# Retention's output product as block pairs of seven products, with the gates ahead of it and weight sums made partly by DMA

## The chip, the cores and the metric

One Trainium2 chip; the kernel runs on one of its cores. The metric is the device time of one execution in microseconds, the median of several runs. TensorE multiplies, VectorE and ScalarE do the elementwise work, SyncE (SP) starts nearly all the DMAs, and GpSimd (POOL) starts some in the changed kernel.

## The reference

Two layers on 512 tokens of width 1024, all float32. Cut to what matters here:

```python
h = rmsnorm(x, g_mix)
z = h @ w_in                      # attention q,k,v | retention q,k,v,g | gate_a | gate_b
ya = sliding_window_sink_attention(aq, ak, av, sinks) @ w_a
r = chunkwise_retention(rq, rk, rv)                       # 4 heads of 256 columns
r = r * lax.rsqrt(jnp.mean(r * r, axis=-1, keepdims=True) + EPS)
r = r.reshape(B, S, RET_V) * jax.nn.silu(rg)              # 512 x 1024
yb = r @ w_b                                              # 1024 x 1024
mixed = jax.nn.sigmoid(ga) * ya + jax.nn.sigmoid(gb) * yb
x = x + mixed @ w_out
h2 = rmsnorm(x, g_mlp)
x = x + jnp.square(jax.nn.relu(h2 @ w_up)) @ w_down       # 4096 hidden columns
```

After the second layer a last rmsnorm follows.

## The kernel before

Activations lie transposed: 8 tiles of 128 features by 512 tokens. For accuracy every float32 operand is split into a high and a low part (`split`: ScalarE copies the source into the high part, VectorE subtracts it for the low part, the "remainder"), and `products` makes of each product three matmuls: high by high, high by low and low by high (lines 280, 281 and 282). Weights come in units of 128 x 1024 elements (512 KB). `unit_order` writes their order out by hand. `unit` hands out the next one and sees to it that the next two are split (`split_until`), which in turn sees to loads further ahead (`load_until`). Loads go into three `raw` tiles, splits into three pairs of `hi` and `lo` tiles, so a load waits on SP's queue until the tile's last reader is done. The order of the instructions on each engine's queue is settled by a scheduler when the kernel is built; each queue then runs in order.

Three shapes of loop use the units. `group` fills four banks of PSUM at once, with the eight input tiles k as its outer loop; `chunk` makes one output tile of 512 tokens from one unit (24 matmuls of 512 columns); `two_chunks` makes two from two units. There are five banks for products.

`pair` makes two output tiles of `w_up` (256 output features by 512 tokens) by a 2 x 2 block scheme with seven products of blocks instead of eight: the blocks are 512 input features by 256 tokens, each product is 4 x 3 matmuls of 256 columns, and three banks a, e and b gather them. Its inputs are blocks of x and four sums of blocks of x (`sum_input`: four additions or subtractions on VectorE, then a split, for each half of the features), its weights are seven blocks, of which some are sums. `load_part` loads the two units of a pair and `add_part` forms the sums with four additions on VectorE of 512 columns each, in `raw` and in large temporary tiles (`big`). A pair comes as four parts for `unit`: three full ones and a half.

The order within a layer, from the retention on: the last values of the retention; `w_in` chunks for the retention's gate (`put_rg`) and for the first four gates `gb` (`gate`), with the retention's second half of the heads woven in between (`advance`, `drain`); a `group` of `w_b`; four more gate chunks; four chunks of `w_b`. `put_mixed` multiplies the result by the gate, adds the attention's share (kept in x's place) and splits the sum into slots `ms`. Then x is loaded back by DMA, from the input or from a copy in DRAM (`spill`), and a group and four chunks of `w_out` add to it. `put_x` also scales and splits each tile of x for the MLP (`scaled_input`, into `xh` and `xl`, with which all products of `w_in` and `w_up` work) and adds up its squares. The MLP begins with a `group` of `w_up`, with `sum_input` and the norm's statistics in its hooks, then two pairs; then 24 turns of a `two_chunks` of `w_down` and a pair in the two layers together; at the end comes a group and chunks of `w_down`.

Of the kernel before, what the change touches and what calls it, by code (L numbers as in the profile page):

```python
# [48 lines left out]
DELAY = 2  # L49


def unit_order():

    order = [("w_in", i) for i in range(4 + 2 + 8 + 2 + 4 + 2)]
    order += [("w_in", i) for i in range(22, 26)]
    order += [("w_a", i) for i in range(4)]
    order += [("w_in", i) for i in range(26, 42)]
    order += [("w_b", i) for i in range(4)]
    order += [("w_in", i) for i in range(42, 46)]
    order += [("w_b", i) for i in range(4, 8)]  # L60
    order += [("w_out", i) for i in range(8)]
    for what, q, i in mlp_sequence():
        if what == "first":
            order += [("w_up", u) for u in range(4)]
        elif what == "pair":
            order += [("pair", 8 * q + 2 * i, part) for part in range(4)]
# [48 lines left out]
def decoder(ctx, tc, xT, x_first, w_in, w_a, w_b, w_out, w_up, w_down, tables, decay, band, out):  # L115
# [17 lines left out]
    def big(name, dtype=F32):  # L133
        return tmp.tile([P, 2, T], dtype, tag="big", name=name, bufs=6)
# [27 lines left out]
    def raw_tile():  # L162
        return wpool.tile([P, UNIT], F32, tag="raw", name="raw")
# [28 lines left out]
    def load_part(i):  # L192
        layer, _, j, part = order[i]
        if part == 0:
            raws[i] = raw_tile()
            nc.sync.dma_start(raws[i][:, LEFT], w_up[layer, j][:, LEFT])
            raws[i + 3] = raw_tile()
            nc.sync.dma_start(raws[i + 3], w_up[layer, j + 1])
        elif part == 1:
            raws[i] = big("raw2").rearrange("p a t -> p (a t)")  # L200
            nc.sync.dma_start(raws[i][:, RIGHT], w_up[layer, j][:, RIGHT])

    def add_part(i):
        part = order[i][3]
        if part == 0:
            w2 = raws[i + 3]
            nc.vector.tensor_tensor(raws[i][:, RIGHT], w2[:, RIGHT], w2[:, LEFT], ALU.add)
        elif part == 1:
            w1 = raws[i - 1]
            nc.vector.tensor_tensor(raws[i][:, LEFT], w1[:, RIGHT], w1[:, LEFT], ALU.subtract)  # L210
        elif part == 2:
            raws[i] = big("raw3").rearrange("p a t -> p (a t)")
            w1, w2, z2 = raws[i - 2], raws[i + 1], raws[i - 1]
            nc.vector.tensor_tensor(raws[i][:, LEFT], w1[:, LEFT], w2[:, RIGHT], ALU.subtract)
            nc.vector.tensor_tensor(raws[i][:, RIGHT], z2[:, RIGHT], z2[:, LEFT], ALU.subtract)

    def split_until(n):
        while state["split"] < min(n, len(order)):
            i = state["split"]
            load_until(i + 3)  # L220
# [10 lines left out]
            for at in (LEFT,) if paired and order[i][3] == 3 else halves(i):  # L231
# [5 lines left out]
            raws.pop(i - 3 if paired else i, None)  # L237
# [76 lines left out]
    def chunk(name, layer, moving, evacuate, rate=1.0):  # L314
# [6 lines left out]
        products(ps, pairs[: n // 2], True, False)  # L321
        advance(rate)
        products(ps, pairs[n // 2 :], False, True)
        evacuate(ps)

    def group(name, layer, moving, evacuates, meanwhile=None):
# [3 lines left out]
        for u in range(4):  # L330
            hi, lo = unit(name, layer)
            for j in range(2):
                k = 2 * u + j
                for c, ps in enumerate(banks):
                    cols = slice(j * T + c * P, j * T + (c + 1) * P)
                    products(ps, [((hi[:, cols], lo[:, cols]), moving[k])], k == 0, k == KD - 1)
# [5 lines left out]
    def two_chunks(name, layer, moving, evacuates):  # L342
# [9 lines left out]
        for ps, evacuate in zip(banks, evacuates):  # L352
            evacuate(ps)

# [125 lines left out]
    def layer_body(layer):  # L480
# [276 lines left out]
        rg, rg_next = {}, {}  # L757

        def put_rg(i):
            def put(ps):  # L760
                if i % 2 == 0:
                    two = big("z")
# [14 lines left out]
        ret = {}  # L777
# [7 lines left out]
        class Head:  # L785
# [53 lines left out]
            def finish(self):  # L839
                h = self.h  # L840
                for e in range(2):
# [5 lines left out]
                    ret[2 * h + e] = (hi, lo)  # L847
# [69 lines left out]
        def gate_tile(c):  # L917
            if c % 2 == 0:
                two = big("gb")
                gates.extend(two[:, j, :] for j in range(2))  # L920

        for c in range(4):
            gate_tile(c)
            chunk("w_in", layer, xs, gate(gates[c]))
        drain()


        ms = {}

        def put_mixed(c):  # L930
            def put(ps):
                m = temp("m")
                nc.vector.tensor_tensor(m, ps, gates[c], ALU.mult)
                nc.vector.tensor_tensor(m, m, mixed[c], ALU.add)
                hi, lo = slots.one(), slots.one()
                split(view(hi), view(lo), m)
                ms[c] = (hi, lo)

            return put

        rT = [tuple(view(s) for s in ret[k]) for k in range(KD)]
        group("w_b", layer, rT, [put_mixed(c) for c in range(4)])
        for c in range(4, KD):
            gate_tile(c)
            chunk("w_in", layer, xs, gate(gates[c]))
        for c in range(4, KD):
            chunk("w_b", layer, rT, put_mixed(c))
        for k in range(KD):
            slots.give(*ret.pop(k))
# [3 lines left out]
        for c in range(KD):  # L953
# [10 lines left out]
        mT = [tuple(view(s) for s in ms[k]) for k in range(KD)]  # L964
# [3 lines left out]
        for k in range(KD):  # L968
            slots.give(*ms.pop(k))
# [5 lines left out]
        H = T // 2  # L975
        sums = [slots.four() for _ in range(4)]
        by_form = [t[0].rearrange("p a (b t) -> p (a b) t", t=H) for t in sums]

        def sum_input(ks):
# [6 lines left out]
            (b11, b12), (b21, b22) = ((t[:, :, :H], t[:, :, H:]) for t in b)  # L986
            f = [big("sums").rearrange("p a (b t) -> p (a b) t", t=H) for _ in range(2)]
            t1, t2, t3, t4 = f[0][:, 0:2, :], f[0][:, 2:4, :], f[1][:, 0:2, :], f[1][:, 2:4, :]
            hi, lo = by_form[ks // 2], by_form[2 + ks // 2]
            nc.vector.tensor_tensor(t1, b12, b11, ALU.subtract)  # L990
            nc.vector.tensor_tensor(t2, b22, t1, ALU.subtract)
            split(hi[:, 0:4, :], lo[:, 0:4, :], f[0])
            nc.vector.tensor_tensor(t3, b22, b12, ALU.subtract)
            nc.vector.tensor_tensor(t4, b21, t2, ALU.subtract)
            split(hi[:, 4:8, :], lo[:, 4:8, :], f[1])

        def form(j):
            return [tuple(by_form[2 * i + k // 2][:, 2 * j + k % 2, :] for i in range(2)) for k in range(4)]

        def block(half, tokens):  # L1000
            at = slice(tokens * H, tokens * H + H)
            return [(xh[:, k, at], xl[:, k, at]) for k in range(4 * half, 4 * half + 4)]
# [20 lines left out]
        def pair(q):  # L1023
            def multiply(ps, weights, left, moving, start=True):
                hi, lo = weights
                cols = [slice((0 if left else 4 * P) + k * P, (0 if left else 4 * P) + (k + 1) * P) for k in range(4)]
                products(ps, [((hi[:, c], lo[:, c]), m) for c, m in zip(cols, moving)], start, True, not start)

            a, e, b = (bank(ps_mm, "mm")[:, :H] for _ in range(3))
            eu, z = temp("eu"), big("z")
            part = unit("pair", layer)
            multiply(a, part, True, block(0, 0))
            nc.scalar.activation(b, a, AF.Copy)  # L1037
            multiply(e, part, False, form(0))
            nc.scalar.activation(eu[:, :H], e, AF.Copy)
            part = unit("pair", layer)  # L1040
            multiply(b, part, True, form(1), False)
            nc.scalar.activation(eu[:, H:], b, AF.Copy)
            multiply(a, part, False, block(1, 0), False)
            nc.vector.scalar_tensor_tensor(z[:, 0, :H], a, 0.0, rms_mlp.value[:, :H], ALU.max, ALU.mult)  # L1044
            part = unit("pair", layer)
            multiply(b, part, True, form(2), False)
            nc.vector.tensor_tensor(z[:, 1, H:], b, eu[:, :H], ALU.add)
            multiply(e, part, False, block(1, 1), False)
            nc.vector.tensor_tensor(z[:, 0, H:], e, eu[:, H:], ALU.add)
            part = unit("pair", layer)  # L1050
            multiply(b, part, True, form(3), False)
            later = rms_mlp.value[:, H:].unsqueeze(1).broadcast_to([P, 2, H])
            nc.vector.scalar_tensor_tensor(z[:, :, H:], z[:, :, H:], 0.0, later, ALU.max, ALU.mult)
            nc.vector.scalar_tensor_tensor(z[:, 1, :H], b, 0.0, rms_mlp.value[:, :H], ALU.max, ALU.mult)
            hi, lo, own = up_home()
            for i in range(2):
# [197 lines left out]
```

## Time and profile before

| | |
|---|---|
| time, median of 3 runs | 1512.68 us (1511.04 to 1513.27) |
| span of the profiled execution | 1511.4 us; the page gives no other time for this execution |
| TensorE busy | 1499.2 us (99%), 8080 matmuls |
| VectorE busy | 1026.7 us (68%) |
| ScalarE busy | 740.1 us (49%) |
| POOL busy | 2.9 us |
| moved by DMA | 155.10 MB, mean 103 GB/s |
| granted clock | 0.998 |

Busy shares are means over the span; what bounds a stage is read from windows, and from the waits in them. [...] In a view of groups a row has the line, the engine, the operation, the tile written and those read, the shape, the count, then busy time and mean duration, and behind the second bar the idle time just before and what ended it. In a view of waits a row has the waiting line, what it waited for, the total, the number and the longest.

### The profile page before, as it was taken

The numbers are of one execution on the slowest core, as the hardware profiler recorded it, in microseconds if no ns is written. First come the engines' busy times: TensorE is split into PE (matmuls) and PEld (weight loads), VectorE is DVE, ScalarE is ACT, GpSimd is POOL, SyncE is SP. The second block draws the span as 40 slices with busy tenths as digits, with TensorE's granted clock in tenths as the row PEclk, the third lists the DMA queues.
The fourth block names the chain that finished last, engine by engine and source line by source line (L and its number), as shares of the span: only waits on it lengthen the run. The fifth ranks groups of instructions, "written<-read, shape, count | busy, mean of one in ns | idle before, by whom it ended". The sixth has DMA issues, their size and how long they took to land.

```text
span 1511.4 us, 20498 instructions
## 1 busy us (share of the span) xinstructions
PE 1499.2 (99%) x8080; PEld 1302.2 (86%) x8080; DVE 1026.7 (68%) x1598; ACT 740.1 (49%) x1163; POOL 2.9 (0%) x13
## 2 busy tenths in 40 slices
PE   9999999999999999999999999999999999999997
PEld 7888888888888999989888888888888999889997
DVE  6877668754787666676678765777449866666664
ACT  6656455632564444444455742555327544444452
POOL 0000000000000000000000000000000000000000
PEclk9999999999999999999999999999999999999999
DMA  6422322233223232233442222222342232232331
GB/s 217 123 97 75 98 79 91 70 125 126 98 78 104 98 112 97 93 104 115 165 131 93 84 84 98 82 79 84 126 125 98 85 104 92 99 111 98 103 108 56
DMA packets 52640, 155.10 MB, mean 103 GB/s; under 512 B 6208, under 2 KB 8384, under 8 KB 52544
## 3 DMA queue, kind: packets, MB, share of 16 engines
q1 hardware_dynamic: 52400, 153.54, 30.6%
q8 instruction: 63, 1.03, 0.3%
q14 instruction: 33, 0.27, 0.1%
q10 hardware_dynamic: 144, 0.26, 0.0%
HBM read 146.96 MB, written 4.19 MB: 100 GB/s over the span
## 4 chain that ended last, share of the span: by engine, by line
PE 98%; ACT 1%; DVE 0%; DMA 0%; issue 0%; DVEq 0%
PE mm L280 29%; PE mm L281 29%; PE mm L282 29%; PE rv L280 2%; PE rv L281 2%; PE rv L282 2%; PE score L651 1%; PE pT L616 1%; PE r L281 1%; PE r L282 1%; PE r L280 1%; PE pv L637 0%; PE pv L636 0%; PE ssq L374 0%; PE ret L281 0%; PE ret L282 0%
## 5 line engine op out<-in xcount | busy, mean ns | idle before, releaser
L235 ACT ACTIVATE hi<-raw 128x1024 fp32r<-128x1024 f32 (+1 forms) x313 | 314.6, 1013 | 517.9 <-PE mm L281 430.6
L236 DVE TENSOR_TENSOR lo<-raw,hi 128x1024 fp32r<-128x1024 f32 (+1 forms) x314 | 362.6, 1164 | 162.0 <-ACT hi L235 161.1
L281 PE MATMUL mm<-r,hi 128*128 128x512 f32 (+1 forms) x1136 | 392.5, 346 | 0.0
L280 PE MATMUL mm<-r,hi 128*128 128x512 f32 (+1 forms) x1136 | 389.5, 346 | 1.0 <-ACT mm L1037 1.0
L282 PE MATMUL mm<-r,lo 128*128 128x512 f32 (+1 forms) x1136 | 388.5, 346 | 0.0
L280 PE MATMUL mm<-xh,hi 128*128 128x512 f32 (+1 forms) x1008 | 358.2, 357 | 0.9 <-ACT xh L290 0.9
L281 PE MATMUL mm<-xl,hi 128*128 128x512 f32 (+1 forms) x1008 | 356.8, 356 | 0.0
L282 PE MATMUL mm<-xh,lo 128*128 128x512 f32 (+1 forms) x1008 | 355.4, 356 | 0.0
L280 PEld LDWEIGHTS mm<-r,hi 128*128 128x128 f32 x1136 | 214.8, 189 | 27.8 <-ACT mm L1037 1.4
L281 PEld LDWEIGHTS mm<-r,hi 128*128 128x128 f32 x1136 | 215.3, 189 | 26.3
L282 PEld LDWEIGHTS mm<-r,lo 128*128 128x128 f32 x1136 | 215.0, 189 | 25.7
L280 PEld LDWEIGHTS mm<-xh,hi 128*128 128x128 f32 x1008 | 191.1, 190 | 27.1 <-ACT xh L290 1.6
L281 PEld LDWEIGHTS mm<-xl,hi 128*128 128x128 f32 x1008 | 191.3, 190 | 25.5
L282 PEld LDWEIGHTS mm<-xh,lo 128*128 128x128 f32 x1008 | 191.0, 190 | 25.5
L1064 DVE TENSOR_TENSOR x<-x,mm 128x512 f32<-128x512 f32 x56 | 37.8, 687 | 34.2 <-PE mm L282 34.2
L282 PE MATMUL rv<-hi,xl 128*128 128x512 f32 x128 | 49.8, 389 | 0.0
L281 PE MATMUL rv<-lo,xh 128*128 128x512 f32 x128 | 49.8, 389 | 0.0
L280 PE MATMUL rv<-hi,xh 128*128 128x512 f32 x128 | 49.4, 391 | 0.0
L281 PE MATMUL mm<-ulo,hi 128*128 128x512 f32 (+1 forms) x128 | 46.3, 363 | 0.0
L280 PE MATMUL mm<-uhi,hi 128*128 128x512 f32 (+1 forms) x128 | 46.2, 362 | 0.0
L282 PE MATMUL mm<-uhi,lo 128*128 128x512 f32 (+1 forms) x128 | 45.7, 365 | 0.0
L1044 DVE SCALAR_TENSOR_TENSOR z<-mm,rstd 128x256 f32<-128x256 f32 x28 | 11.9, 425 | 42.0 <-PE mm L282 42.0
(188 smaller groups left out, 1682.1 us busy)
## 6 DMA issues: line engine op xcount, KB each, us to landing
raw<-w_in_in SPq DMA_DIRECT2D x89, 512.0 KB, 3.3
raw<-w_down_in SPq DMA_DIRECT2D x64, 512.0 KB, 3.3
raw<-w_up_in SPq DMA_DIRECT2D x36, 512.0 KB, 3.3
raw<-w_up_in SPq DMA_DIRECT2D x56, 256.0 KB, 2.7
raw<-w_b_in SPq DMA_DIRECT2D x16, 512.0 KB, 3.2
raw<-w_out_in SPq DMA_DIRECT2D x16, 512.0 KB, 3.5
raw<-w_a_in SPq DMA_DIRECT2D x8, 512.0 KB, 3.3
x<-xT_in SPq DMA_DIRECT2D x15, 256.0 KB, 3.6
```

Source lines behind the costliest of these rows:

```text
L235: nc.scalar.activation(hi[:, at], raw[:, at], AF.Copy)
L236: nc.vector.tensor_tensor(lo[:, at], raw[:, at], f32(hi[:, at]), ALU.subtract)
L280: nc.tensor.matmul(ps, ah, bh, start=start and i == 0, stop=False, **more)
L281: nc.tensor.matmul(ps, ah, bl, start=False, stop=False, **more)
L282: nc.tensor.matmul(ps, al, bh, start=False, stop=stop and i == n - 1, **more)
L616: nc.tensor.transpose(pt[:, i * P : (i + 1) * P], sm[:, at : at + P], ident)
L651: nc.tensor.matmul(ps[:, g * w : (g + 1) * w], q_s[g][:, c, at], part[:, keys], start=i == 0, stop=i == 1)
L1044: nc.vector.scalar_tensor_tensor(z[:, 0, :H], a, 0.0, rms_mlp.value[:, :H], ALU.max, ALU.mult)
L1064: nc.vector.tensor_tensor(x[:, c, :], x[:, c, :], ps, ALU.add)
```

## The change

The product with `w_b` no longer runs as a group and four chunks, but as four pairs of output tiles with the scheme of seven products that the MLP uses; so `pair` is made general, and what is done with its banks is given by a `Sink` (`Up` for the MLP, `Mixed` here). For it the retention's result before its split is kept (`zs`), and `Forms`, made from `sum_input`, forms the four sums of its blocks between the gate chunks. All eight gate chunks come ahead of the pairs. `Mixed` writes the split sum into `xh` and `xl`, which the gates were the last to read; the products of `w_out` read it there, its group with the input tiles in the order in which the pairs make them (`OUT_TILES`). The splits of x for the MLP, which go into the same tiles, can only follow the last chunk of `w_out`, and are made there behind each product (`used`).

The signs in the scheme are turned so that each sum of weight blocks is an addition. Per pair, two of the four are made by VectorE (`add_part`, parts 1 and 2) and two by accumulating DMAs on POOL's queue on top of a plain load (`load_part`, parts 0 and 2). Some blocks are loaded twice for it: 1792 KB for a pair where it was 1024 KB. This holds for the 28 pairs of the MLP and the 8 of `w_b`. There are five `raw` tiles instead of three, loads start four units ahead of a split instead of three, and eight `big` tiles instead of six; the space reserved for POOL's DMA descriptors is 2048 bytes of a partition. The layouts of the weights in DRAM follow.

```diff
+AHEAD = 4
+B_PAIRS = (0, 4, 2, 6)
+OUT_TILES = (0, 1, 4, 5, 2, 3, 6, 7)
...
-    order += [("w_in", i) for i in range(26, 42)]
-    order += [("w_b", i) for i in range(4)]
-    order += [("w_in", i) for i in range(42, 46)]
-    order += [("w_b", i) for i in range(4, 8)]
+    order += [("w_in", i) for i in range(26, 46)]
+    order += [("pair", "w_b", c, part) for c in B_PAIRS for part in range(4)]
...
     def load_part(i):
-        layer, _, j, part = order[i]
+        layer, _, name, j, part = order[i]
+        two = [weights[name][layer, j + a] for a in range(2)]
+        raws[i] = raw = raw_tile()
         if part == 0:
-            raws[i] = raw_tile()
-            nc.sync.dma_start(raws[i][:, LEFT], w_up[layer, j][:, LEFT])
-            raws[i + 3] = raw_tile()
-            nc.sync.dma_start(raws[i + 3], w_up[layer, j + 1])
+            nc.sync.dma_start(raw, two[0])
+            nc.gpsimd.dma_start(raw[:, RIGHT], two[1][:, LEFT], accum_op=ALU.add)
         elif part == 1:
-            raws[i] = big("raw2").rearrange("p a t -> p (a t)")
-            nc.sync.dma_start(raws[i][:, RIGHT], w_up[layer, j][:, RIGHT])
+            nc.sync.dma_start(raw[:, RIGHT], two[1][:, RIGHT])
+        elif part == 2:
+            nc.sync.dma_start(raw[:, LEFT], two[0][:, LEFT])
+            nc.gpsimd.dma_start(raw[:, LEFT], two[0][:, RIGHT], accum_op=ALU.add)
+        else:
+            nc.sync.dma_start(raw[:, LEFT], two[1][:, LEFT])

     def add_part(i):
...
+        if order[i][4] in (1, 2):
+            last = raws.pop(i - 1)
+            at = LEFT if order[i][4] == 1 else RIGHT
+            nc.vector.tensor_tensor(raws[i][:, at], last[:, LEFT], last[:, RIGHT], ALU.add)
...
-            load_until(i + 3)
+            load_until(i + AHEAD)
...
+    def pair(layer, tiles, form, sink):
...
+        a, e, b = (bank(ps_mm, "mm")[:, :H] for _ in range(3))
+        eu = temp("eu")
+        part = unit("pair", layer)
+        multiply(a, part, True, block(tiles, 0, 0))
+        nc.scalar.activation(b, a, AF.Copy)
+        multiply(e, part, False, form[0])
+        nc.scalar.activation(eu[:, H:], e, AF.Copy)
+        part = unit("pair", layer)
+        multiply(b, part, True, form[1], False)
+        nc.scalar.activation(eu[:, :H], b, AF.Copy)
+        multiply(a, part, False, block(tiles, 1, 0), False)
+        sink.one(a)
+        sink.two(eu)
+        part = unit("pair", layer)
+        multiply(b, part, True, form[2], False)
+        sink.three(b, eu[:, H:])
+        multiply(e, part, False, block(tiles, 1, 1), False)
+        sink.four(e, eu[:, :H])
+        part = unit("pair", layer)
+        multiply(b, part, True, form[3], False)
+        sink.done(b)
...
+        ret_sums = Forms()
         for c in range(4, KD):
-            gate_tile(c)
-            chunk("w_in", layer, xs, gate(gates[c]))
-        for c in range(4, KD):
-            chunk("w_b", layer, rT, put_mixed(c))
+            if c < 6:
+                ret_sums.add(2 * c - 8, (zs.pop(c - 4), zs.pop(c - 2)))
+            gated(c)
...
+        class Mixed(Sink):
...
+            def one(self, a):
+                nc.vector.tensor_tensor(self.m[:, 0, :H], a, self.gate[:, 0, :H], ALU.mult)
+
+            def three(self, b, eu):
+                nc.vector.scalar_tensor_tensor(self.m[:, 1, H:], b, -1.0, eu, ALU.mult, ALU.subtract)
+
+            def four(self, e, eu):
+                nc.vector.tensor_tensor(self.m[:, 0, H:], e, eu, ALU.add)
+
+            def done(self, b):
+                m, two = self.m, slice(self.c, self.c + 2)
+                nc.vector.scalar_tensor_tensor(m[:, 1, :H], b, -1.0, self.gate[:, 1, :H], ALU.mult, ALU.mult)
+                nc.vector.tensor_tensor(m[:, :, H:], m[:, :, H:], self.gate[:, :, H:], ALU.mult)
+                nc.vector.tensor_tensor(m, m, x[:, two, :], ALU.add)
+                split(xh[:, two, :], xl[:, two, :], m)
+
+        rT = [ret[k] for k in range(KD)]
+        for c in B_PAIRS:
+            pair(layer, rT, ret_sums, Mixed(c))
...
             def put(ps):
                 nc.vector.tensor_tensor(x[:, c, :], x[:, c, :], ps, ALU.add)
-                scaled_input(c, g_mlp)
                 squared_input(c, g_mlp)
...
-        group("w_out", layer, mT, [put_x(c) for c in range(4)])
+        group("w_out", layer, xs, [put_x(c) for c in range(4)], tiles=OUT_TILES)
         for c in range(4, KD):
-            chunk("w_out", layer, mT, put_x(c))
+            chunk("w_out", layer, xs, put_x(c), used=(lambda k: scaled_input(k, g_mlp)) if c == KD - 1 else None)
...
-    nc = bacc.Bacc("TRN2", target_bir_lowering=False, num_devices=1)
+    nc = bacc.Bacc("TRN2", target_bir_lowering=False, num_devices=1, dynamic_dma_scratch_size=2048)
```

More of the change, by code (lines that the diff above doesn't have):

```diff
@@ L65, in unit_order @@
         elif what == "pair":
-            order += [("pair", 8 * q + 2 * i, part) for part in range(4)]
+            order += [("pair", "w_up", 8 * q + 2 * i, part) for part in range(4)]
         elif what == "down":
@@ L230, in split_until @@
                 lo = wpool.tile([P, UNIT], F32R, tag="lo", name="lo")
[L231 removed]
+            for at in (LEFT,) if paired and order[i][4] == 3 else halves(i):
                 if i == 0 and at.start == 0:
@@ L321, in chunk @@
         products(ps, pairs[: n // 2], True, False)
+        for k in range(n // 2 if used else 0):
+            used(k)
         advance(rate)
@@ L324, in chunk, with group @@
         evacuate(ps)
-    def group(name, layer, moving, evacuates, meanwhile=None):
+        for k in range(n // 2, n if used else 0):
+            used(k)
+    def group(name, layer, moving, evacuates, meanwhile=None, tiles=range(KD)):
         banks = [bank(ps_mm, "mm") for _ in range(4)]
@@ new lines, in block, with two, multiply @@
+    def block(tiles, half, tokens):
+        at = slice(tokens * H, tokens * H + H)
+        return [(hi[:, at], lo[:, at]) for hi, lo in tiles[4 * half : 4 * half + 4]]
+    class Sink:
+        def one(self, a):
+            pass
+        def two(self, eu):
+            pass
+        def three(self, b, eu):
+            pass
+        def four(self, e, eu):
+            pass
+        def done(self, b):
+            pass
+    def pair(layer, tiles, form, sink):
+        def multiply(ps, weights, left, moving, start=True):
+            hi, lo = weights
+            cols = [slice((0 if left else 4 * P) + k * P, (0 if left else 4 * P) + (k + 1) * P) for k in range(4)]
+            products(ps, [((hi[:, c], lo[:, c]), m) for c, m in zip(cols, moving)], start, True, not start)
+        a, e, b = (bank(ps_mm, "mm")[:, :H] for _ in range(3))
[19 more added lines that the diff above has]
+        sink.done(b)
@@ L915, in layer_body, with gated @@
         gates = []
-        def gate_tile(c):
+        def gated(c):
             if c % 2 == 0:
-                two = big("gb")
-                gates.extend(two[:, j, :] for j in range(2))
+                gates.append(big("gb"))
+            chunk("w_in", layer, xs, gate(gates[c // 2][:, c % 2, :]))
         for c in range(4):
-            gate_tile(c)
-            chunk("w_in", layer, xs, gate(gates[c]))
+            gated(c)
         drain()
[L928 to L939, printed above, removed]
@@ L941, in layer_body @@
-        rT = [tuple(view(s) for s in ret[k]) for k in range(KD)]
-        group("w_b", layer, rT, [put_mixed(c) for c in range(4)])
-        for c in range(4, KD):
-            gate_tile(c)
-            chunk("w_in", layer, xs, gate(gates[c]))
-        for c in range(4, KD):
-            chunk("w_b", layer, rT, put_mixed(c))
-        for k in range(KD):
-            slots.give(*ret.pop(k))
+        ret_sums = Forms()
+        for c in range(4, KD):
+            if c < 6:
+                ret_sums.add(2 * c - 8, (zs.pop(c - 4), zs.pop(c - 2)))
+            gated(c)
@@ L985, in sum_input @@
                     nc.scalar.activation(b[part][:, i, :], x[:, g, :], AF.Copy, scale=gain[:, col : col + 1])
[L986 to L1002, printed above, removed]
+            sums.add(ks, b)
         up = [[] for _ in range(4)]
@@ L1021, in up_home @@
             return big("uhi", F32R), big("ulo", F32R), []
[L1023 to L1056, printed above, removed]
-                nc.scalar.activation(z[:, i, :], z[:, i, :], AF.Square)
-                split(hi[:, i, :], lo[:, i, :], z[:, i, :])
-                up[q].append((hi[:, i, :], lo[:, i, :]))
-            up_slots[q].extend(own)
@@ L1082, in layer_body @@
             elif what == "pair":
-                pair(q)
+                pair(layer, xs, sums, Up(q))
                 if (q, i) == (3, 3):
-                    for t in sums:
-                        slots.give(*t[1])
+                    sums.free()
             elif what == "down":
```

119 lines of the change are left out of this document (84 added, 35 removed).

## The prediction

> **What bounds the kernel now.** I read the page first, then the waits of TensorE, then the windows around the output product of the retention.
>
> ```profile
> span 1511.4 us, 20498 instructions
> ## 1 busy us (share of the span) xinstructions
> PE 1499.2 (99%) x8080; PEld 1302.2 (86%) x8080; DVE 1026.7 (68%) x1598; ACT 740.1 (49%) x1163; POOL 2.9 (0%) x13
> ...
> PE 98%; ACT 1%; DVE 0%; DMA 0%; issue 0%; DVEq 0%
> ```
> ```profile
> PE mm L280 <- ACT mm L1037: 1.0, 2, 0.5
> PE mm L280 <- ACT xh L290: 0.9, 1, 0.9
> ```
> ```profile
> 0.00:20.00 20.00, 18.02 (x62) 14.13 (x63) 15.02 (x25) 16.07 (x27) 1.94 (x12) 1.00 0.84 296
> 300.00:325.00 25.00, 25.00 (x112) 20.72 (x111) 11.81 (x14) 8.67 (x10) 0.00 (x0) 1.00 0.27 88
> 351.00:372.00 21.00, 21.00 (x95) 17.38 (x94) 10.73 (x15) 6.15 (x7) 0.00 (x0) 1.00 0.43 137
> 392.00:412.00 20.00, 20.00 (x90) 16.57 (x89) 18.56 (x26) 17.27 (x26) 0.00 (x0) 1.00 0.27 94
> 412.00:433.00 21.00, 21.00 (x95) 17.38 (x94) 20.18 (x24) 10.95 (x13) 0.00 (x0) 1.00 0.27 89
> ```
>
> TensorE is the path: 98% of the chain, and in the middle of the kernel its waits are two of 0.5 us. (Columns of a window: length, busy us of PE, PEld, DVE, ACT and POOL with counts, granted clock, DMA share, GB/s.) The w_b product (300 to 325 its group, 351 to 372 its chunks) has no TensorE gap at all, and the clock is full. So time is won only by fewer or shorter matmuls, and lost only where some other engine now comes later than TensorE. VectorE is the one without room: 18.56 of 20 us and 20.18 of 21 us busy in the chunks of w_out and the first w_up group behind them.
>
> **TensorE's work.** The price of a matmul is the step from one start to the next, not its listed duration. First the 512-column form (12 steps, 11 rows left out), then the 256-column form of a pair (73 steps):
>
> ```profile
> 289.70 0.39 PE L280 MATMUL mm<-xh,hi 128*128 128x512 f32 x1
> ...
> 292.42 0.39 PE L280 MATMUL mm<-xh,hi 128*128 128x512 f32 x1
> ```
> ```profile
> 441.21 0.28 PE L280 MATMUL mm<-xh,hi 128*128 128x256 f32 x1
> ...
> 449.95 0.28 PE L281 MATMUL mm<-r,hi 128*128 128x256 f32 x1
> ```
> ```profile
> 498.71 0.46 PE mm L282 x2
> ...
> 519.71 0.46 PE mm L282 x2
> ```
>
> 2.72/12 = 0.227 us and 8.74/73 = 0.120 us. Two output tiles of w_b cost 2 x 8 x 3 = 48 wide matmuls, 10.88 us; as a pair of seven products they cost 7 x 4 x 3 = 84 narrow ones, 10.06 us by the step. The chain checks it: one MLP turn (48 wide and one pair) is 519.71 - 498.71 = 21.00 us, which leaves the pair 10.12. The gain is 0.76 to 0.82 us a pair; there are four pairs in each of two layers, so 6.1 to 6.6 us. I take 6.2. [...] Everything else that TensorE does is moved, not changed: four gate chunks change places with the w_b group, at nothing, since both run gapless.
>
> **VectorE in the w_b pairs.** Steps of VectorE, when it is full:
>
> ```profile
> 410.41 0.69 DVE L990 TENSOR_TENSOR sums<-xg 128x512 f32<-128x512 f32 x1
> 411.02 1.22 DVE L236 TENSOR_TENSOR lo<-raw,hi 128x1024 fp32r<-128x1024 f32 x1
> 412.15 1.22 DVE L288 TENSOR_TENSOR r<-sums,r 128x1024 fp32r<-128x1024 f32 x1
> 413.29 0.75 DVE L291 SCALAR_TENSOR_TENSOR xl<-x,xh 128x512 fp32r<-128x512 f32 x1
> ```
> ```profile
> 445.52 0.42 DVE L1049 TENSOR_TENSOR z<-mm,eu 128x256 f32<-128x256 f32 x1
> 445.86 0.41 DVE L1047 TENSOR_TENSOR z<-mm,eu 128x256 f32<-128x256 f32 x1
> ```
> ```profile
> L235 ACT ACTIVATE hi<-raw 128x1024 fp32r<-128x1024 f32 x280 | 293.9, 1058 | 497.9 <-PE mm L281 410.6 <-issue 64.4 <-PE rv L282 14.5
> ```
>
> So 0.61, 1.13 and 0.34 us for 512, 1024 and 256 columns. A w_b pair needs five of 1024 (three weight remainders, the addition of x's mixed tile, the split of the result), four of 512 (half a remainder, two weight additions, the gate) and four of 256: 5.65 + 2.44 + 1.36 = 9.45 us against 10.1 on TensorE. ScalarE needs some 6 (three 1.06 for weights, half of one more, one for the result, three small copies). VectorE is 94% full, four pairs long, but not the bound. The forms of the retention's result (8 additions and 4 splits, 4.9 + 4.5 = 9.4 us a layer) lie under the four gate chunks (4 x 24 x 0.227 = 21.8 us) beside four gates and four to six remainders (some 8 us): hidden. The last pair's result (0.34 + 1.13 + 1.06 + 1.13 = 3.7 us behind its last product) is hidden because w_out reads tiles 6 and 7 last, 6 x 12 x 0.227 = 16.3 us into its group; without that order it would cost 3.7 us a layer. In the MLP each of 28 pairs loses two additions, 1.2 us of VectorE that nobody waits for: nothing gained.
>
> **The accumulating DMAs.** There are 72 (two for each of 36 pairs, 256 KB each) on the queue of POOL, which does nothing else then. Each waits for a plain load of the same bytes, and VectorE's weight addition waits for it, with everything that is queued behind that addition: remainders, evictions, the reciprocal. The trace of before has none. Nearest rows:
>
> ```profile
> raw<-w_up_in SPq DMA_DIRECT2D x36, 512.0 KB, 3.3
> raw<-w_up_in SPq DMA_DIRECT2D x56, 256.0 KB, 2.7
> ...
> spill<-x SPq DMA_DIRECT2D x8, 256.0 KB, 2.0
> x<-spill SPq DMA_DIRECT2D x8, 256.0 KB, 2.7
> raw<-w_in_in SPq DMA_DIRECT2D x5, 256.0 KB, 5.8
> ```
>
> Call A the time from the moment the plain load has landed to the moment the sum has landed. It can't be under 2.7 (a plain load of that size), and twice that size's slowest row, 11.6, is the upper end. I take 4.7, near the lower row: a load of 256 KB and another 2.0 us, the row of a plain write of as much, for going over the destination. [...] In the w_b pairs the DMAs move 1792 KB of weights and 512 KB of x in 10.1 us, 234 GB/s; the first 20 us moved 296, so the engines can carry it, though landings may grow.
>
> How much A may be, read from the order of the changed kernel's instructions and the steps above, counted by hand:
> In the MLP a pair's first load is issued when the previous pair's second part is split, about 2.3 us after a w_down unit ends on TensorE; it lands 3.3 later; behind its sum stand the addition, an eviction, another addition and the next w_down remainder (0.6 + 0.3 + 0.6 + 1.1, 0.2 for semaphores), which TensorE needs 15.5 us after that unit's end. Free up to A = 7.1.
> In w_b the addition for pair three stands ahead of the remainders of pair two's last parts; issued 2.3 us into pair one, and 3.8 us of VectorE's work from there to what TensorE needs at 15.8: free up to A = 6.4.
> Behind the first w_up group the addition for the second MLP pair stands ahead of the reciprocal. Here is that place before:
>
> ```profile
> 422.30 1.22 DVE L236 TENSOR_TENSOR lo<-raw,hi 128x1024 fp32r<-128x1024 f32 x1
> ...
> 427.91 3.35 DVE L376 RECIPROCAL rstd<-rstd 128x512 f32<-128x512 f32 x1 [0.78 <-ACT rstd L375]
> ...
> 434.29 1.37 DVE L1009 SCALAR_TENSOR_TENSOR up<-mm,rstd 128x512 f32<-128x512 f32 x2 [0.65 <-PE mm L282]
> ```
>
> The reciprocal ends 3 us ahead of the evictions of w_up, which free the banks that the first pair needs. The change takes these 3 us: all eight splits of x move behind the last w_out chunk's products (0.66 us each; six of them were done by then), some 4 us more on VectorE, less three weight additions (1.8). The fourth w_up remainder then ends near 424.3; load 3.3, sum A, addition 0.6, reciprocal 3.3, one remainder 1.1, and the first eviction must be there when the pair's second product starts, near 437.6. Free up to A = 4.3; beyond, a microsecond of A is a microsecond of TensorE, once a layer. At 4.7 that is 0.4 a layer, 0.8 in all. The first x split itself (ScalarE 0.7, VectorE 0.7 from the first product of the last chunk) is ready just about when the w_up group begins: nothing, at worst 1 us a layer.
>
> **Sum.** Against the profiled execution: 1511.4 - 6.2 + 0.8 = 1506.0 us of span. The page gives no time around the span; the median of the runs is 1.3 us above it, and I leave that. So 1507.3 us. A measurement of this kernel can tell about 0.2%, 3 us, from no change.
>
> **Rivals.**
> Part of the gain is eaten: A between 5.8 and 7, which the 5.8 us row under a loaded queue speaks for. At 5.8 the w_up place costs 1.5 a layer, at 7 2.7 and w_b another 0.6 for two pairs: 1509.5 to 1514. Chance 0.17.
> The sums land late: A over 7.1. Then the MLP waits too, in each of 24 pairs that follow a w_down, and the weight additions become the pace. At A = 8, 24 x 0.9 for the MLP, 2 x (3.7 + 2 x 1.6) for the rest: 21.6 + 13.8 - 6.2 = 29 us slower, 1542; at 7.3 some 9 slower, 1522. For it: nothing in the trace shows an addition in a DMA. Against: POOL is empty, DMA share is 0.27 to 0.43 in these windows. Chance 0.22. [...]
> More is won, because the 0.5 us waits at the first pair go (the copy of a into b now stands earlier on ScalarE) and the steps shrink: 1504 to 1505.5. Chance 0.03.
> The forecast keeps 0.58.
>
> **Numbers.** Forecast and its neighbours give 1505.5 to 1509.5. The range goes to 1520, which takes in the second case and the start of the third; left out are some 0.15 of the third and 0.03 below. Faster by over 0.2% (under 1509.7): 0.61. Same: 0.16. Slower (over 1515.7): 0.23.
>
> **What would show it.** Right: 8368 matmuls; pairs of w_b 10.1 us apart; sums from POOL landing in 3.5 to 5.5 us; TensorE busy near 1493 and gaps of a microsecond at most around the first MLP pair. Wrong: VectorE idle ahead of weight additions and released by a DMA, TensorE released by remainders in w_b or MLP turns over 21.0 us.

## The result and the profile after

The changed kernel takes 1561.05 us (1553.5 to 1566.42) where the kernel before, on the same chip, takes 1512.76: ratio 1.032, 95% interval 1.029 to 1.0351. It is slower by 48 us, where 1507.3 was forecast, and far above the range.

First the page of the changed kernel: span, busy times, the shares of the chain that ended last, and the group of the weight additions on VectorE (behind the second bar: idle just before them, and what ended it).

```profile
span 1564.6 us, 21566 instructions
...
PE 1510.0 (97%) x8368; PEld 1316.1 (84%) x8368; DVE 1032.9 (66%) x1606; ACT 765.8 (49%) x1203; POOL 65.5 (4%) x85
...
PE 74%; DMA 11%; DVE 9%; issue 5%; ACT 2%; DVEq 0%; POOLq 0%
...
L212 DVE TENSOR_TENSOR raw<-raw 128x512 f32<-128x512 f32 x72 | 49.7, 690 | 140.4 <-DMA raw<-w_up_in 91.2
```

TensorE had 98% of the chain before; now 74%, and DMA has 11%. The weight additions take 50 us, and VectorE sits idle for 140 us ahead of them. TensorE's own waits (total, times, longest) show what that does to it, and the landings from issue (KB each, median us) show the transfers.

```profile
PE mm L280 <- DVE lo L233: 38.1, 24, 3.5
PE mm L278 <- DVE up L1090: 4.0, 2, 2.2
```
```profile
raw<-w_up_in SPq DMA_DIRECT2D x84, 256.0 KB, 2.7
raw<-w_up_in SPq DMA_DIRECT2D x36, 512.0 KB, 4.4
raw<-w_up_in POOLq DMA_DIRECT2D x56, 256.0 KB, 4.1
...
raw<-w_b_in POOLq DMA_DIRECT2D x16, 256.0 KB, 4.7
```

TensorE waits for weight remainders (`lo`) 24 times, 38 us in all, and for the evictions behind the first `w_up` group 2.0 us a layer. The sums themselves land as fast as forecast (4.1 and 4.7 us, where 3.5 to 5.5 was forecast).

Where a turn of the MLP goes from 21 to 24 us is seen in the chain of waits of one turn of the first layer (start, length, what; from the first matmuls of a `w_down` unit that need its remainder to those of the next turn's):

```profile
580.30 1.05 PE mm L280 x2
...
585.83 0.23 PE mm L280
586.05 0.34 PE mm L278 x2
...
587.63 1.07 ACT hi L232
...
589.87 1.23 DVE lo L233
...
591.12 4.57 DMA raw<-w_up_in
...
596.36 4.59 DMA raw<-w_up_in
...
601.02 0.09 DVE raw L212
...
601.63 0.70 DVE lo L233
...
602.96 0.42 DVE z L1112
603.38 1.14 DVE lo L233
...
604.57 0.74 PE mm L280 x2
```

It is a ring that closes on itself. The `w_down` unit runs to 586.05; then comes the half product of the pair, which the scheduler has put behind this unit; then the tiles of weights become free and two units are split (587.63 to 591.10). That releases a `raw` tile, and only then does the next pair's plain load start (591.12). POOL starts the sum at 596.36, VectorE has it at 601.02, and addition, remainder, a second addition, an eviction and the next `w_down` remainder bring TensorE to 604.57: 24.27 us round, where a turn of the kernel before takes 21.0. (Some 1.7 us of it are TensorE's own: up to 583.7 its steps are 0.43 us instead of 0.23; see the last section.)

### The profile page after: what moved, and what is told of

It reads as the page before. It is cut to its first block, busy times and chain, and to the rows that moved or that the text cites. A ratio compares the mean times of both kernels' runs of the same rounds, so it can differ in the third digit from the quotient of the medians.

```text
span 1564.6 us, 21566 instructions
## 1 busy us (share of the span) xinstructions
PE 1510.0 (97%) x8368; PEld 1316.1 (84%) x8368; DVE 1032.9 (66%) x1606; ACT 765.8 (49%) x1203; POOL 65.5 (4%) x85
## 3 DMA queue, kind: packets, MB, share of 16 engines
q0 software_dynamic: 10368, 18.88, 7.7%
## 4 chain that ended last, share of the span: by engine, by line
PE 74%; DMA 11%; DVE 9%; issue 5%; ACT 2%; DVEq 0%; POOLq 0%
PE mm L280 21%; PE mm L278 21%; PE mm L279 21%; DMA raw<-w_up_in 8%; DVE lo L233 5%; DMA raw<-w_b_in 2%; PE rv L278 2%; PE rv L279 2%; PE rv L280 2%; ACT hi L232 1%; PE score L743 1%; PE pT L708 1%; PE r L279 1%; PE r L280 1%; PE r L278 1%
## 5 line engine op out<-in xcount | busy, mean ns | idle before, releaser
L279 PE MATMUL mm<-xl,hi 128*128 128x512 f32 (+1 forms) x1136 | 407.1, 360 | 1.0 <-DVE xl L289 0.9
L278 PE MATMUL mm<-xh,hi 128*128 128x512 f32 (+1 forms) x1136 | 405.2, 361 | 0.9 <-ACT xh L288 0.9
L280 PE MATMUL mm<-xh,lo 128*128 128x512 f32 (+1 forms) x1136 | 404.1, 360 | 0.1
L280 PE MATMUL mm<-r,lo 128*128 128x256 f32 (+1 forms) x1104 | 358.1, 329 | 37.8 <-DVE lo L233 37.6
L278 PE MATMUL mm<-r,hi 128*128 128x256 f32 (+1 forms) x1104 | 356.4, 326 | 4.3 <-DVE up L1090 4.0
L279 PE MATMUL mm<-r,hi 128*128 128x256 f32 (+1 forms) x1104 | 359.1, 326 | 0.0
L279 PEld LDWEIGHTS mm<-xl,hi 128*128 128x128 f32 x1136 | 215.5, 190 | 32.2 <-DVE xl L289 1.9
L278 PEld LDWEIGHTS mm<-xh,hi 128*128 128x128 f32 x1136 | 215.4, 190 | 32.0 <-ACT xh L288 1.6
L280 PEld LDWEIGHTS mm<-xh,lo 128*128 128x128 f32 x1136 | 215.4, 190 | 30.9 <-DVE lo L233 0.5
L212 DVE TENSOR_TENSOR raw<-raw 128x512 f32<-128x512 f32 x72 | 49.7, 690 | 140.4 <-DMA raw<-w_up_in 91.2
L1127 ACT ACTIVATE z<-z 128x512 f32<-128x512 f32 x56 | 35.0, 625 | 62.2 <-DVE z L1123 61.9
```

What stands on the lines that cost most here:

```text
L212: nc.vector.tensor_tensor(raws[i][:, at], last[:, LEFT], last[:, RIGHT], ALU.add)
L278: nc.tensor.matmul(ps, ah, bh, start=start and i == 0, stop=False, **more)
L279: nc.tensor.matmul(ps, ah, bl, start=False, stop=False, **more)
L280: nc.tensor.matmul(ps, al, bh, start=False, stop=stop and i == n - 1, **more)
L1127: nc.scalar.activation(z[:, i, :], z[:, i, :], AF.Square)
```

## The experiments

The time of the kernel before was 1511.4 to 1513.0 in these runs. All ratios are to it.

| what runs | us, median | ratio, 95% interval |
|---|---|---|
| all sums on VectorE | 1510.61 | 0.9993 (0.9983 to 1.0003) |
| sums by DMA in the MLP only | 1551.5 | 1.0259 (1.0238 to 1.0279) |
| sums by DMA in `w_b` only | 1521.61 | 1.0061 (1.0041 to 1.0081) |
| POOL's DMAs without the addition | 1522.51 | 1.007 (1.0051 to 1.0088) |
| plain load in halves | 1559.35 | 1.0313 (1.0295 to 1.0332) |
| more lead in the MLP | 1522.59 | 1.0067 (1.0047 to 1.0088) |
| that lead, `w_b` by VectorE | 1511.55 | 0.9998 (0.9989 to 1.0007) |
| the same, one unit of lead | 1515.63 | 1.0024 (1.0012 to 1.0035) |
| the same, other tiles alone | 1514.32 | 1.0019 (1.0009 to 1.0028) |
| one of `w_b`'s two sums by DMA | 1520.5 | 1.0052 (1.0039 to 1.0064) |
| that sum by POOL's adder | 1511.66 | 1.0002 (0.9993 to 1.0011) |
| VectorE, and freer `raw` tiles | 1512.18 | 1.0001 (0.9992 to 1.001) |

### Are the sums by DMA the whole loss, and in which stage?

All weight sums on VectorE, nothing on POOL's queue; no block is loaded twice then:

```diff
+    BY_DVE = ('w_b', 'w_up')
...
+        if name in BY_DVE:
...
+            if part == 0:
+                nc.sync.dma_start(raws[i], two[0])
+                raws[i + 3] = raw_tile()
+                nc.sync.dma_start(raws[i + 3][:, LEFT], two[1][:, LEFT])
...
+            return
...
+        if order[i][4] == 0 and order[i][2] in BY_DVE:
+            w1, w2 = raws[i], raws[i + 3]
+            nc.vector.tensor_tensor(raws[i + 2][:, LEFT], w1[:, LEFT], w1[:, RIGHT], ALU.add)
+            nc.vector.tensor_tensor(w1[:, RIGHT], w1[:, RIGHT], w2[:, LEFT], ALU.add)
```

> Changed kernel with all weight sums on VectorE (four additions a pair, no DMA on POOL); everything else of the change stays. Theory 1, the round trip: the loss comes from a raw tile's way round (remainder done, load, sum by DMA, addition, remainder), 24.2 us where a turn has 21.0; without the summing DMAs nothing waits and the 6.2 us of the matmuls remain: 1505 to 1510 us. Theory 2, the rest of the change (the w_b pairs with VectorE 94% full, the late splits of x, the new order) makes the loss: over 1540 us.

Its busy times, TensorE's wait for remainders, and the window over the first layer's `w_b` pairs (length, busy us of PE, PEld, DVE, ACT and POOL with counts, granted clock, DMA share, GB/s):

```profile
PE 1492.9 (99%) x8368; PEld 1309.9 (87%) x8368; DVE 1075.3 (71%) x1678; ACT 770.3 (51%) x1203; POOL 2.9 (0%) x13
```
```profile
PE mm L296 <- DVE lo L249: 3.5, 5, 0.8
```
```profile
325.00:366.00 41.00, 39.97 (x326) 39.27 (x325) 37.61 (x52) 21.59 (x32) 0.00 (x0) 1.00 0.49 154
```

1510.61 us, 0.6 over the range of the first theory. All of the loss is gone with the DMAs. TensorE's busy time is 6.3 us under that of before, as the forecast's matmul term says, but the span only 3.0 (1508.4): idle time of TensorE takes the rest. The interval doesn't tell this kernel from the one before.

The same for one product alone: `BY_DVE` holds only `w_b` (the MLP by DMA), then only `w_up` (`w_b` by DMA).

> Only the MLP's pairs keep the summing DMAs, the w_b pairs have their sums on VectorE. Theory 1: the MLP carries the larger part, 26 of the 43 us of new TensorE gaps, so scaled to the whole loss some 36 us, and the first w_up group some 5: 1540 to 1552 us. Theory 2: no nearer to 1507 than the changed kernel, 1555 to 1565.

> Only the w_b pairs keep the summing DMAs, the MLP's sums are on VectorE. Theory 1: w_b's part of the gaps, 12 of 43, scaled to some 16 us: 1518 to 1528 us. Theory 2: 1555 to 1565.

TensorE's waits in the one and in the other:

```profile
PE mm L296 <- DVE lo L249: 27.4, 22, 2.5
PE mm L294 <- DVE up L1106: 4.4, 2, 2.4
```
```profile
PE mm L296 <- DVE lo L249: 10.8, 9, 2.5
```

1551.5 and 1521.61: 40.9 and 11.0 us over all sums on VectorE. The two add up to 51.9, and the changed kernel is 50.4 over it. The MLP has four fifths of the loss, `w_b` one fifth; a third part, if there is one, is smaller than the spread of the changed kernel's own runs (1553.5 to 1566.42).

### Is it the price of the addition, the rate of the DMAs, or the lead?

POOL's DMAs as plain ones, which leaves one addend out of each of these sums:

```diff
-            nc.gpsimd.dma_start(raw[:, RIGHT], two[1][:, LEFT], accum_op=ALU.add)
+            nc.gpsimd.dma_start(raw[:, RIGHT], two[1][:, LEFT])
```

> As changed, but POOL's DMAs overwrite and do not add (the sums of weights lack one addend). It tells whether the addition or the queue is dear. If the addition makes the difference between 2.7 us (plain, SP) and 4.1 to 4.7 (POOL, adding): POOL's DMAs land in about 2.7 to 3.2 and a turn is 1.4 us shorter, 1520 to 1535 us. If POOL's queue does: they land in 4 us as before, 1555 to 1566 us.

Its queue of POOL (packets, MB, share of 16 engines) and its landings, then that queue in the changed kernel:

```profile
q0 software_dynamic: 5760, 18.88, 3.8%
...
raw<-w_up_in POOLq DMA_DIRECT2D x56, 256.0 KB, 3.2
...
raw<-w_b_in POOLq DMA_DIRECT2D x16, 256.0 KB, 3.3
```
```profile
q0 software_dynamic: 10368, 18.88, 7.7%
```

1522.51 us: landing 0.9 to 1.4 us sooner (the medians) wins 38.5 us. The 24 full turns of the MLP have a mean of 21.28 us instead of 22.48, so 1.2 us a turn, 29 us in all: what the sum lands sooner comes off the turn nearly whole, as it must where the sum is on the path. The turns are not quite back at 21.0, so the addition is a part of the shortage and not all of it.

The plain load in two halves, the half that the sum goes onto first:

```diff
-            nc.sync.dma_start(raw, two[0])
+            for at in (RIGHT, LEFT):
+                nc.sync.dma_start(raw[:, at], two[0][:, at])
```

> As changed, but a pair's first plain load comes as two of 256 KB, the half to which POOL adds first, so that the sum waits for 256 KB and not for 512. Theory 1, the round trip: in the changed kernel 5.2 us of the 24.2 us of a bad turn are that load; with some 3 us in its place a turn is 2 us shorter, which is about all that a turn loses on the average (38 us in 24 turns): 1518 to 1532 us. If what bounds is the rate of the DMA engines and not the way round: no change, 1555 to 1566.

A miss: 1559.35, no gain that can be told from the spread of the changed kernel's runs, and the time that was expected if the rate of the DMA engines were the bound; the next run speaks against that. The loads of 256 KB of `w_up` land here in 3.4 us (median of 140), where those of the changed kernel took 2.7, so a half saves some 1 us of the 4.4 and not 2. The evictions that begin the MLP's second and last pair in the first layer (`z`, 256 columns), in the changed kernel and in this one:

```profile
460.76 0.42 DVE L1112 SCALAR_TENSOR_TENSOR z<-mm,rstd 128x256 f32<-128x256 f32 x1 [0.83 <-PE mm L280]
...
735.06 0.42 DVE L1112 SCALAR_TENSOR_TENSOR z<-mm,rstd 128x256 f32<-128x256 f32 x1 [1.64 <-PE mm L280]
```
```profile
461.04 0.42 DVE L1113 SCALAR_TENSOR_TENSOR z<-mm,rstd 128x256 f32<-128x256 f32 x1 [0.83 <-PE mm L281]
...
727.65 0.42 DVE L1113 SCALAR_TENSOR_TENSOR z<-mm,rstd 128x256 f32<-128x256 f32 x1 [1.65 <-PE mm L281]
```

These twelve turns take 274.3 us in the changed kernel and 266.6 here: the later ones are shorter (most by 0.4 to 1.7 us), but the first one is 3.8 us longer, and the second layer's twelve turns, the first of them 3.2 longer, win nothing. This is one execution of each. Why the first turn suffers was not settled.

More lead for the MLP, with the same adding DMAs: the tiles of parts 0 and 2 come from the pool of `big` tiles instead of `raw`, and loads are issued up to three units earlier where the `raw` tiles allow it.

```diff
-        raws[i] = raw = raw_tile()
+        wide = name == "w_up" and part in (0, 2)
+        raws[i] = raw = big("rawb").rearrange("p a t -> p (a t)") if wide else raw_tile()
...
-            load_until(i + AHEAD)
+            load_until(i + ahead(i))
```

> As changed, but in the MLP the two tiles of a pair that POOL adds to come from the eight large temporary tiles, which stand idle there, and loads start up to three units earlier. Same DMAs, same sums. Theory 1: the round trip gets some 5 us or more of slack and the MLP's stalls go, w_b's and those at the first w_up group stay: 1515 to 1530 us. Theory 3, the summing DMAs hold up the DMA engines so that all loads land late whatever their lead: 1550 to 1565 us.

1522.59. Every MLP turn behind the first pairs is 21.0 to 21.2 us again, though the sums land no faster (4.5 us). So with more lead neither the rate nor the addition in itself holds the MLP back. What is left is `w_b`, and putting that on VectorE as well should take it away; two more kernels divide the remedy, one with a single unit of lead and one with none, so that the other tiles alone remain:

> The MLP's loads as in the run with more lead (tiles p0 and p2 from another pool, loads up to three units earlier, the same adding DMAs), w_b's sums on VectorE. If the loss is two separate shortages of lead, one in the MLP and one in w_b, both are gone: MLP turns of 21.0 and w_b as with all sums on VectorE, 1508 to 1513. If the two stages share a cost that either remedy only moved, 1515 to 1525.

> As the run before it, but with loads at most one unit earlier than in the changed kernel instead of three. The shortage in a turn is 2 to 4 us and a unit of w_down is 5.4 us: if that is the whole shortage, the turns are at 21.0 and the time is 1508 to 1513; if the loads need the full distance, 1520 to 1545.

> As the run before it, but with no unit of lead in the order of issue: only the tiles of p0 and p2 come from the other pool. If the plain load waited for the release of the raw tile, the wait goes with that and the time is 1508 to 1520; if the place in the order of issue holds it back, the time stays with that of only the MLP by DMA, 1540 to 1552.

1511.55, 1515.63 and 1514.32. The first and the third came out as the lead says; the second lies between its two bands, 2.6 us over the lower one: in its profile three turns of the second layer and one of the first are 21.3 to 22.1, and why these is open. In the source, the kernel with the other tiles alone differs from the one of only the MLP by DMA (1551.5) in nothing but the pool from which two of four tiles come, and so leaves the five `raw` tiles to the rest; the adding DMAs and the blocks that are loaded twice stay. It is 37 us faster. One of its turns, the rows of SP's queue, POOL and VectorE:

```profile
521.29 0.45 SPq L211 DMA_DIRECT2D rawb<-w_up_in  x1
```
```profile
527.16 0.86 POOL L212 DMA_DIRECT2D rawb<-w_up_in  x1 [7.04 <-DMA rawb<-w_up_in]
```
```profile
532.02 0.69 DVE L229 TENSOR_TENSOR raw<-rawb 128x512 f32<-128x512 f32 x1 [3.64 <-issue]
...
536.72 0.42 DVE L1140 SCALAR_TENSOR_TENSOR z<-mm,rstd 128x256 f32<-128x256 f32 x1 [0.47 <-PE mm L308]
```

Counted back from that eviction, the load is issued 15.4 us ahead (536.72 - 521.29), where it was 11.8 in the turn shown above (602.96 - 591.12). Load with start of the sum (5.9 us) and sum (4.9) take, if anything, longer than there (5.2 and 4.7). VectorE still waits for DMAs, nearly as long as in the changed kernel:

```profile
DVE raw L229 <- DMA rawb<-w_up_in: 88.4, 18, 6.3
```

But the addition begins 4.7 us ahead of the eviction instead of 1.9, and TensorE waits for nothing in this turn; what waits for remainders are left in the MLP (4.6 us in all) lie at its first pairs, in the first turn of the second layer and at its end. So the load's wait for a `raw` tile is what the MLP's loss hung on.

### One sum in `w_b`

All on VectorE again, but part 2's sum in `w_b` by DMA instead of on VectorE; and then the same sum on POOL's own adder, without a DMA:

```diff
+            elif part == 2 and name == "w_b":
+                nc.sync.dma_start(raws[i][:, LEFT], two[0][:, LEFT])
+                nc.gpsimd.dma_start(raws[i][:, LEFT], two[0][:, RIGHT], accum_op=ALU.add)
```
```diff
-            nc.vector.tensor_tensor(raws[i + 2][:, LEFT], w1[:, LEFT], w1[:, RIGHT], ALU.add)
+            adder = nc.gpsimd if order[i][2] == "w_b" else nc.vector
+            adder.tensor_tensor(raws[i + 2][:, LEFT], w1[:, LEFT], w1[:, RIGHT], ALU.add)
```

> As with all sums on VectorE, but in the w_b pairs the sum for the third part is made by a DMA on POOL (a plain load of 256 KB under it). With all sums on VectorE that stage had VectorE busy 37.61 of 41 us and TensorE waited 3.5 us in all for remainders. If VectorE's load is what these waits come from: they go, 1506 to 1509 us. If the DMA's way round is too long here too (it has 8 pairs only): 1511 to 1518.

> As with all sums on VectorE, but in the w_b pairs the same sum is made by POOL's own adder instead, with no DMA more. If POOL takes at most some 2 us for 512 columns and does not slow VectorE: 1506 to 1509 us. If it is slow or holds VectorE up: 1510 to 1520.

1520.5 and 1511.66. With the DMA the time is over both ranges that were expected. It is now ScalarE that comes late, because the copy into the high part waits for the sum, and an eviction that frees a bank is queued behind that copy. TensorE's waits, and ScalarE's:

```profile
PE mm L298 <- ACT eu L451: 5.6, 3, 3.0
PE mm L300 <- DVE lo L253: 3.1, 5, 0.7
```
```profile
ACT hi L252 <- DMA raw<-w_b_in: 19.4, 4, 6.5
```

One sum by DMA costs 10 us there, nearly what two cost (11.0). The other run takes a 0.69 us addition off VectorE in each `w_b` pair and wins nothing, but VectorE then waits for POOL's slower addition (2.28 us on average; twice, 2.4 us in all), and TensorE waits 4.2 us for remainders instead of 3.5. So it doesn't tell whether VectorE's load in these pairs is what keeps the kernel with all sums on VectorE from the full 6.3 us.

### Late `raw` tiles in the kernel with all sums on VectorE?

```diff
-                raws[i] = raw_tile()
+                wide = name == "w_up" and part == 2
+                raws[i] = big("rawb").rearrange("p a t -> p (a t)") if wide else raw_tile()
```

> All sums on VectorE as in the first run, and in the MLP the tile of p2 from the other pool, so that the next loads find a raw tile sooner. TensorE was busy 6.3 us less there than before the change, but the time fell by 2.3 us. If late raw tiles cost the rest (the last w_down loads, the first turn of the MLP), 1507 to 1509.5; if they do not, 1510 to 1512.

1512.18: no gain. The remaining 3.3 us of that kernel stay without a proven cause; with all sums on VectorE, TensorE waits five times for remainders, up to 0.8 us, twice in the pairs of `w_b`, twice where the MLP begins and once at its end. No version beats the kernel before by more than a measurement can tell.

## Why the prediction was wrong

**TensorE's work: right.** -6.2 us forecast, -6.3 in busy time with all sums on VectorE, with the same 8368 matmuls.

**VectorE in the `w_b` pairs: not the bound, but not tested at its forecast load.** The 94% was for two weight additions a pair; in the changed kernel VectorE waits there for the sums. With all four additions on it, it is busy for 37.61 of 41 us, 92%, and TensorE loses 1.0 us there.

**A, the landing of the sum: near.** 4.7 was taken, counted from the landing of the plain load. In the turn shown that load lands at 595.69 (591.12 + 4.57) and VectorE has the sum at 601.02, so A is 5.3: 0.67 to the start on POOL and 4.66 from there.

**The step that failed is "free up to A = 7.1" for the MLP.** It put three terms against 15.5 us from a `w_down` unit's end to the next `w_down` remainder: issue after 2.3, load 3.3, and 2.8 behind the sum; 15.5 - 8.4 = 7.1. In the turn shown they measure 5.1 (586.05 to 591.12), 4.6 (to 595.69) and 3.6 (601.02 to 604.57): 13.2. TensorE's rows show when it needed the remainder:

```profile
602.80 0.40 PE L279 MATMUL mm<-r,hi 128*128 128x512 f32 x1
604.57 0.74 PE L280 MATMUL mm<-r,lo 128*128 128x512 f32 x2 [1.37 <-DVE lo L233]
```

It had work until 603.2, 17.1 us after 586.05, because the half product now lies in this stretch and four matmuls of the next unit need only its high part. So 17.1 - 13.2 = 3.9 was free; A = 5.3 is 1.4 late, which is the wait in the second row. Together with the 1.7 us of slower steps that is most of the way from 21.0 to this turn's 24.3 (this is one of the longer turns; all 24 full turns of both layers have a mean of 22.5).

The largest part is the release, 2.8 us: I counted the load from the place where the program issues it, one split after the unit's end. SP's queue held it until a `raw` tile was free, and for that the half product had to run and two units had to be split. The scheduler's move of the half product behind the first `w_down` unit could be seen in the order of instructions; I counted from the order in the source. (The same move puts off the need by the half product's 1.4 us, so half of the 2.8 comes back.) The load is 1.3: I took the median of 512 KB loads from a kernel that never had them on its path (3.3). The 0.8 behind the sum are nearly all a remainder of 512 columns (601.63, 0.70 us) that I did not have between the two additions. A itself is 0.6.

**"Sums land late" was the right mechanism with the wrong point from which it decides.** As that rival says, the MLP waits in the pairs that follow a `w_down` and the weight additions set the pace. Its condition, A over 7.1, was not met; A was 5.3, and the limit 3.9 in the turn shown. By its price per turn (24 turns, 22.5 - 21.0) it is 36 us for the MLP, and the runs give 40.9 with the start of the MLP. That start (forecast 0.4 us a layer) measures 2.0 in TensorE's waits.

In `w_b` the limit of 6.4 failed in the same way, as read from the trace of the first layer; no run tested that limit by itself. The first pair begins at 327.10. The load for pair three goes out 4.6 us later and not 2.3, and load and sum together take 11.8 us (to 343.42), where 3.3 + 4.7 was taken and 3.3 + 6.4 was free:

```profile
331.67 0.33 SPq L198 DMA_DIRECT2D raw<-w_b_in  x1
343.42 0.69 DVE L212 TENSOR_TENSOR raw<-raw 128x512 f32<-128x512 f32 x1 [4.65 <-DMA raw<-w_b_in]
347.37 0.39 PE L280 MATMUL mm<-r,lo 128*128 128x256 f32 x1 [3.49 <-DVE lo L233]
```

TensorE waits 3.5 us there. The forecast had no loss in `w_b`; the sums by DMA there cost 11.0.

**Busy time was a term I didn't have.** 1493 was forecast for TensorE; 1510.0 came, for the same matmuls. So the loss against all sums on VectorE, 56.2 us of span, is some 39 of waits (45.8 against 6.3 when all of TensorE's waits are added) and 17 of busy time. The last section has about half of these 17.

## What to carry to other kernels

A transfer's lead is counted from the release of its buffer in the built order of the queues, not from its place in the program (here 5.1 us behind the `w_down` unit's end, not 2.3); each stage put in series behind it (a second DMA and its start on another queue, here 5.3 us) comes out of the same lead. In a kernel whose loads run in a ring with the work, the first remedy to try is another buffer for just the tiles on the ring: here it gave back 37 of 41 us with no transfer made faster. And a sum that costs an engine 0.69 us is worth moving to a DMA only where that engine is what is waited for, which it hardly was here.

## What the runs showed of the hardware

**The granted clock fell behind some waits of TensorE and not behind others.** TensorE's rows in the turn shown, its first matmuls after a wait of 1.95 us, and the window of 4 us behind it; then the same in an earlier turn with a wait of 2.35 us:

```profile
580.30 1.05 PE L280 MATMUL mm<-r,lo 128*128 128x512 f32 x2 [1.95 <-DVE lo L233]
581.15 0.63 PE L278 MATMUL mm<-r,hi 128*128 128x512 f32 x1
```
```profile
534.33 0.73 PE L280 MATMUL mm<-r,lo 128*128 128x512 f32 x2 [2.35 <-DVE lo L233]
```
```profile
534.00:538.00 4.00, 3.67 (x16) 3.04 (x17) 3.46 (x6) 1.26 (x2) 0.86 (x1) 1.00 0.48 111
...
580.00:584.00 4.00, 3.69 (x9) 2.91 (x10) 3.43 (x6) 1.26 (x2) 0.00 (x0) 0.57 0.66 138
```

In the same 4 us TensorE began 9 matmuls instead of 16, at a granted clock of 0.57; some 3.4 us after the wait (580.30 to 583.7) the steps are 0.23 again. The longer wait before didn't do it, so it is not the length alone. In the whole execution there are five such stretches of 3.4 to 3.5 us at a clock of 0.50 or 0.51, at waits of 1.8 to 3.5 us; at five other waits of 2.0 to 3.4 us there is none. Two of the other stretches:

```profile
348.40:351.80 3.40, 3.40 (x18) 3.40 (x17) 2.60 (x5) 0.45 (x2) 0.00 (x0) 0.50 0.88 321
1136.90:1140.30 3.40, 3.40 (x18) 3.40 (x17) 3.26 (x5) 1.01 (x1) 0.00 (x0) 0.50 0.67 224
```

What decides whether the clock falls is not shown by these runs. The mean granted clock is 0.993 against 0.998 with all sums on VectorE, which by estimate is 0.005 x 1564.6 = 8 us of the 17 of busy time; five stretches of 3.4 us at half the clock give about as much. The rest was not traced to a cause.

**What POOL's transfers and adder cost.** In the changed kernel 256 KB of `w_up` or `w_b` land in 2.7 us (median) from SP's queue and in 4.1 to 4.7 from POOL's with the addition; as plain DMAs POOL's landed in 3.2 to 3.3. With the addition the queue has 10368 packets, without it 5760, for the same 18.88 MB. The same addition of 512 columns took 0.69 us on VectorE and on average 2.28 on POOL:

```profile
L224 POOL TENSOR_TENSOR raw<-raw 128x512 f32<-128x512 f32 x8 | 18.2, 2278 | 730.5 <-DVE lo L250 730.5
```
